# Layer 0's first adaLN shifts on VectorE and its scales on TensorE; the output projection's operands and first tiles made beside the last filter piece

## The chip, the cores and the metric

The kernel runs on one core of a Trainium2 chip. The metric is the device time of one execution in microseconds (us), the median over runs. A core has TensorE (PE in the profile, with its weight loads as PEld), VectorE (DVE), ScalarE (ACT), GpSimd (POOL) and SyncE (SP), which here only issues DMAs. Each works through its own instructions in order and waits on semaphores for the others. All times below are in microseconds from the start of the profiled execution.

## The reference, cut to what matters

A two-layer encoder trunk on a sequence of 1024 tokens with 1024 channels. Layer 0 mixes attention and an RWKV-7 scan, layer 1 is a Hyena operator whose long filters depend on weights alone.

```python
cond = jax.nn.silu(c)
for layer in range(2):
    mod = (cond @ ada_w[layer] + ada_b[layer])[:, None, :]
    shift_m, scale_m, gate_m, shift_f, scale_f, gate_f = jnp.split(mod, 6, axis=-1)
    h = rms_norm(x, norm_mix[layer]) * (1.0 + scale_m) + shift_m
    if layer == 0:
        p = h @ mix_w_in
        y_attn = blocked_gqa(...p...)              # 512 columns
        y_rwkv = rwkv7_bidirectional(...p...)      # 512 columns
        y = jnp.concatenate([y_attn, y_rwkv], axis=-1) @ mix_w_out
    else:
        y = hyena_mixer(h, ...)                    # filters by FFT, from weights alone
    x = x + gate_m * y
    h = rms_norm(x, norm_ffn[layer]) * (1.0 + scale_f) + shift_f
    x = x + gate_f * swiglu(h, ffn_w1[layer], ffn_w3[layer], ffn_w2[layer])
return rms_norm(x, final_norm)
```

The change touches two places of layer 0: `shift_m` and `scale_m` of its first norm, and the first half of the projection by `mix_w_out`, the 512 rows that belong to the attention's output.

## The kernel before

Activations lie in SBUF transposed, as eight tiles of 128 channels by 1024 tokens (`xT`, `h`). The kernel keeps its own stock of SBUF tiles: F32 pages of 128 x 1040 from one end of the memory and F32R pages from the other; `repage(nf, nr)` sets how many there are of each, `page()` takes one and `free()` gives it back, `fence()` sets pages above an index aside. F32R pages hold operands of the large matmuls: every operand is split into a high part (ScalarE, L256) and a low part (VectorE, L257), and `mm3` (L296) multiplies high by high, high by low and low by high. PSUM has eight banks, which `set_banks` divides between two groups. Generators that `yield` are run side by side by `weave`, each with a weight; the order of the program comes from that, and a scheduler of the framework then orders each engine's instructions.

The start: `load_xT` loads x and transposes it on PE (L372). `ada_first` then makes shift (part 0) and scale (part 1) of the first norm: for each half of 512 channels and each part it loads four tiles of `ada_w` (L395) and multiplies each by the condition, as matmuls with one output row (L398, counted twice in the profile, since they are f32). The row is copied (L401), and `ada_cols` turns it into four columns by matmuls with ones (L412), adds the bias (L414) and, for the scale, forms `gs` (L419). All later parts go through `ada_part`, which sums the same products on VectorE in `acc` of 128 x 512 (L441, L443) and lets the ones of L412 sum over the partitions. `norm_h` needs both: L532 multiplies by `gs`, ScalarE (L535) and VectorE (L536) add the shift and split the result. The mixer's first steps then spill x (L206, `sp_x`) and load the input weights (L274). Its first two tiles hold the columns of the decay and learning-rate inputs, whose second products are L1107 and L1109; the weights for these are loaded at L1087.

The end of the mixer: after the input projection, units of the scan (four pairs of heads, two directions; `rwkv_x`, `rwkv_y`, `rwkv_s`, closed by `rwkv_post`) are woven with `other`, which first runs the attention and then `hy_filters`, the filters of layer 1. A filter piece makes taps (PE L1805, ACT L1807, DVE L1808), a first FFT stage (PE L1830, then L1749 to L1751) and, late, an 8-point stage on VectorE (`dft8`, L1699 and L1700), whose result GpSimd stores (L1777). The last stage takes 64 steps of `other` beside the scan's last unit; what is left of it runs alone. Then `repage(13, 33)`, eight loads of x, and `project`: four loads and splits of the attention's outputs (`sp_ya`) and `matvec_add`, which makes for each of eight channel tiles 24 matmuls and two VectorE instructions that add the gated product to x (L801). `ffn` then starts with the second half of the projection, `matvec_halves` (L828), whose operands are the scan's outputs (`sp_yr`).

Of the kernel before, what the change touches and what calls it, by code (L numbers as in the profile page):

```python
# [10 lines left out]
F32 = mybir.dt.float32  # L11
# [65 lines left out]
class Kern:  # L77
# [80 lines left out]

    def free(self, *aps):
        for a in aps:  # L160
            if isinstance(a, (tuple, list)):
                self.free(*a)
            else:
                dt, t, _ = self.page_of[a.tensor.name]
                assert all(t is not q for q in self.pages[dt])
                self.put(t)
# [42 lines left out]
    def unspill(self, d, eng=None):  # L209
        t = self.page()  # L210
        (eng or self.nc.sync).dma_start(out=t, in_=d)
        return t
# [172 lines left out]
    def ada_first(self):  # L385
# [3 lines left out]
        for half in range(2):  # L389
            for part in range(2):  # L390
                c0 = part * D + half * 512
                ps = self.bank()
                for j in range(4):
                    wt = self.page((P, 2, 512))
                    nc.sync.dma_start(out=wt, in_=w[256 * j : 256 * j + 256, c0 : c0 + 512].rearrange("(k p) n -> p k n", p=P))  # L395
                    for i in range(2):
                        k = 2 * j + i
                        nc.tensor.matmul(ps[0:1], self.cond[:, k : k + 1], wt[:, i], start=k == 0, stop=k == 7)  # L398
                    self.free(wt)
                row = self.page((P, 512))  # L400
                nc.scalar.copy(row[0:1], ps[0:1])  # L401
                self.fbank(ps)
                self.ada_cols(0, part, half, row[0:1], 0)
                self.free(row)
# [378 lines left out]
    def matvec_add(self, xT, w, ys, layer, part, g=0, keep=None):  # L783
# [5 lines left out]
        for mp in range(KT // 2):  # L789
# [760 lines left out]
    def mixer(self, w, h, ada):  # L1550
# [120 lines left out]
    def load_mats(self, name):  # L1671

        out = []
        for i in range(2):
            t = self.page((P, 4, 256))
# [78 lines left out]
    def hy_filters(self, g):  # L1754
# [3 lines left out]
        F = self.load_mats("F") + self.load_mats("Fn")  # L1758
# [156 lines left out]
    def hyena(self, w, h, tail):  # L1915
# [140 lines left out]
        def rest():  # L2056
# [5 lines left out]
            for n, _ in enumerate(tail(zs[:4])):  # L2062
                yield 1.0 if n == 0 else 5.3
# [31 lines left out]
def build(ctx, tc, ins, out):  # L2095
# [44 lines left out]
    def project(xT, ys, w, layer, g=0):  # L2140
# [115 lines left out]
```

## Time and profile before

| | before |
|---|---|
| three runs, median | 3384.54 (3375.49 to 3385.33) |
| profiled execution | 3373.19, span 3371.4 |
| mean granted PE clock, profiled execution | 0.963 |
| PE, VectorE, ScalarE, GpSimd busy | 3158.1, 2341.6, 1229.9, 197.0 |
| DMA | 460.24 MB, mean 137 GB/s |

A window's row names its bounds, its length, and per engine the busy time with the count of instructions in brackets; then the granted PE clock, the mean busy share of the 16 DMA engines and their GB/s. A row of the timeline has start, duration, engine, line, operation, output and input, form and count; in brackets at its end stands the idle time of the engine before it and who ended it. A row with "q" behind the engine is an issue, not work. Line numbers in the text are those of the kernel before; in the changed kernel the same lines stand 7 to 19 further down.

### The profile page before, as it was taken

What the parts mean: (1) busy time and instruction counts of PE and PEld (TensorE: products, weight loads), DVE (VectorE), ACT (ScalarE), POOL (GpSimd) and SP (SyncE); (2) the same over time, 40 slices, a digit from 0 to 9 for tenths busy, and PEclk for the clock granted to TensorE, in tenths of its full rate; (3) what the DMA queues carried; (4) which work ended last, traced back from release to release, by engine and by line L of the source; (5) the groups of instructions that cost most, each with busy time, mean ns of one, the idle gap of its engine ahead of it and who ended that gap; (6) DMA issues with size and microseconds to landing.
All of it is one profiled execution on the core that took longest, in us unless ns stands there. A gap on an engine that the chain in (4) does not pass through costs nothing.

```text
span 3371.4 us, 51166 instructions
## 1 busy us (share of the span) xinstructions
PE 3158.1 (94%) x20227; PEld 2554.1 (76%) x20227; DVE 2341.6 (69%) x4011; ACT 1229.9 (36%) x2146; POOL 197.0 (6%) x443
## 2 busy tenths in 40 slices
PE   8899989999989979999999999989977899999998
PEld 4687767776668867888887877877765788888886
DVE  5465565666667895887877665699898686667545
ACT  4632355555554432532233333222120443334211
POOL 2000000000001110000001210000000000000000
PEclk9999999989989999999999999999988999999998
DMA  8654542332334253244449983332446322234311
GB/s 273 220 190 139 158 98 70 84 87 64 76 72 111 98 183 137 94 156 137 147 135 308 352 281 125 100 119 90 148 162 218 132 82 75 77 111 138 122 41 51
DMA packets 331377, 460.24 MB, mean 137 GB/s; under 512 B 101816, under 2 KB 233745, under 8 KB 331136
## 3 DMA queue, kind: packets, MB, share of 16 engines
q1 hardware_dynamic: 292576, 322.04, 31.1%
q0 software_dynamic: 38384, 134.86, 11.4%
q8 instruction: 159, 2.61, 0.3%
q14 instruction: 82, 0.67, 0.1%
q10 hardware_dynamic: 176, 0.07, 0.0%
HBM read 312.71 MB, written 141.56 MB: 135 GB/s over the span
## 4 chain that ended last, share of the span: by engine, by line
PE 58%; DVE 8%; DMA 5%; issue 3%; ACT 2%; POOL 0%; DVEq 0%; SPq 0%; ACTq 0%; POOLq 0%
PE bk L296 21%; PE bk L615 8%; PE bk L616 8%; PE bk L614 8%; PE bk L1830 2%; DVE p L1699 2%; PE bk L1849 2%; DMA p<-in_hy_w_in_dram 1%; DVE p L257 1%; DMA p<-in_ffn_w_dram 1%; PE bk L2002 1%; PE bk L1859 1%; PE bk L1805 1%; PE bk L2025 1%; DMA p<-sp_z 1%
## 5 line engine op out<-in xcount | busy, mean ns | idle before, releaser
L296 PE MATMUL bk<-p,p 128*128 128x512 f32 x5136 | 1235.2, 399 | 75.3 <-ACT p L256 35.0
L296 PEld LDWEIGHTS bk<-p,p 128*128 128x128 f32 x5136 | 974.8, 192 | 299.1 <-ACT p L256 39.3
L256 ACT ACTIVATE p<-p 128x512 fp32r<-128x512 f32 (+3 forms) x542 | 402.6, 758 | 945.8 <-PE bk L615 262.4
L257 DVE TENSOR_TENSOR p<-p,p 128x512 fp32r<-128x512 f32 (+3 forms) x542 | 450.9, 847 | 235.0 <-ACT p L256 189.5
L615 PE MATMUL bk<-p,p 128*128 128x512 f32 x1248 | 485.4, 389 | 3.8 <-DVE p L257 3.8
L614 PE MATMUL bk<-p,p 128*128 128x512 f32 x1248 | 485.0, 390 | 0.1
L616 PE MATMUL bk<-p,p 128*128 128x512 f32 x1248 | 483.8, 389 | 0.0
L615 PEld LDWEIGHTS bk<-p,p 128*128 128x128 f32 x1248 | 234.3, 188 | 53.0 <-DVE p L257 4.7
L614 PEld LDWEIGHTS bk<-p,p 128*128 128x128 f32 x1248 | 234.3, 188 | 48.6 <-ACT p L256 0.5
L616 PEld LDWEIGHTS bk<-p,p 128*128 128x128 f32 x1248 | 234.2, 188 | 48.5
L801 DVE SCALAR_TENSOR_TENSOR p<-bk,mod,p 128x512 f32<-128x512 f32 x192 | 134.9, 744 | 95.0 <-PE bk L296 91.7
L443 DVE SCALAR_TENSOR_TENSOR p<-p,cond,p 128x512 f32<-128x512 f32 x140 | 104.6, 749 | 53.6 <-DMA p<-in_ada_w_dram 51.8
L1699 DVE TENSOR_TENSOR p<-p 128x256 f32<-128x256 f32 (+1 forms) x336 | 130.8, 452 | 0.0
L1830 PE MATMUL bk<-p,p 128*128 128x256 f32 x512 | 125.3, 392 | 5.1 <-DVE p L1751 4.0
L944 DVE TENSOR_REDUCE mx<-bk 128x1 f32<-128x512 f32 x128 | 86.2, 684 | 35.5 <-PE bk L941 34.8
L1830 PEld LDWEIGHTS bk<-p,p 128*128 128x128 f32 x512 | 95.1, 194 | 19.6 <-DVE p L1751 5.1
L1056 ACT COPY p<-bk 128x512 f32<-128x512 f32 (+1 forms) x80 | 43.4, 588 | 169.2 <-DVE p L1876 63.9
L1699 DVE TENSOR_TENSOR p<-p,p 128x1024 f32<-128x1024 f32 (+1 forms) x144 | 91.1, 681 | 18.8 <-ACT p L1850 18.8
L964 ACT COPY p<-bk 128x512 f32<-128x512 f32 x128 | 74.2, 587 | 78.4 <-PE bk L963 75.9
L948 ACT ACTIVATE p<-bk,mx 128x512 f32<-128x512 f32 x128 | 86.9, 686 | 42.3 <-DVE mx L945 41.8
L963 PE MATMUL bk<-k_ident,p 128*128 128x128 f32 x512 | 88.3, 300 | 11.8 <-ACT p L964 9.2
L1362 PEld LDWEIGHTS bk<-p,p 64*64 64x64 f32 x2048 | 73.4, 139 | 29.7 <-issue 15.8
(407 smaller groups left out, 4179.9 us busy)
## 6 DMA issues: line engine op xcount, KB each, us to landing
p<-in_ffn_w_dram SPq DMA_DIRECT2D x120, 512.0 KB, 4.8
p<-in_ada_w_dram SPq DMA_DIRECT2D x96, 512.0 KB, 5.0
sp_f<-p POOLq DMA_DIRECT2D x36, 512.0 KB, 5.5
p<-sp_f POOLq DMA_DIRECT2D x36, 512.0 KB, 5.7
hs<-p POOLq DMA_DIRECT2D x32, 512.0 KB, 3.7
p<-hs SPq DMA_DIRECT2D x32, 512.0 KB, 4.4
p<-sp_r SPq DMA_DIRECT2D x24, 512.0 KB, 5.7
p<-sp_x SPq DMA_DIRECT2D x24, 512.0 KB, 3.6
```

Of the source, the lines that this page charges most:

```text
L256: self.nc.scalar.activation(out=hi, in_=src, func=AF.Copy)
L257: self.nc.vector.tensor_tensor(out=lo, in0=src, in1=hi.bitcast(F32), op=ALU.subtract)
L296: nc.tensor.matmul(ps[n], a, b[:, HALVES[n]], start=s, stop=e)
L443: nc.vector.scalar_tensor_tensor(out=acc, in0=wt[:, i], scalar=self.cond[:, k : k + 1], in1=acc, op0=ALU.mult, op1=ALU.add)
L614: nc.tensor.matmul(ps, op[:, 0, k], mh, start=start and k == 0, stop=False)
L615: nc.tensor.matmul(ps, op[:, 0, k], ml, start=False, stop=False)
L616: nc.tensor.matmul(ps, op[:, 1, k], mh, start=False, stop=stop and k == 3)
L801: nc.vector.scalar_tensor_tensor(out=xs, in0=ps[n], scalar=self.modc(layer, part, m), in1=xs, op0=ALU.mult, op1=ALU.add)
L948: nc.scalar.activation(out=pr[:, HALVES[n]], in_=ps[n], func=AF.Exp, scale=0.125, bias=m[:, 2:3], accum_out=st["s", qt // 4][:, qt % 4, e, ...
L963: nc.tensor.transpose(pt[:, j], pr[:, k * P : (k + 1) * P], self.ident)
L1699: tt = lambda o, a, b, op: nc.vector.tensor_tensor(out=o, in0=a, in1=b, op=op)
L1830: nc.tensor.matmul(ps[j][:, ri], F[2 * d + t2 // 4][:, t2 % 4, 128 * ri : 128 * ri + 128], tp[:, j, d], start=d == 0, stop=d == 1)
```

## The change

In `ada_first` the matmuls L398 stay for the scale alone; the shift is summed on VectorE as in `ada_part`, and the loads of the two parts alternate. The mixer's last stage takes 48 steps of `other` instead of 64, sets pages from 32 on aside, then lowers the stock to 32 F32 pages and raises it to 16 F32R pages, and weaves the rest of `other` with the first six steps of `project`: four loads with their splits, and two tiles. The x tiles of this projection are each loaded at their turn into the lowest free page and kept (`keep`), where before all eight were loaded ahead. The filters' transform matrices are put into low pages too. `project` yields after each split, and the weights of its steps in layer 1 are adapted to that.

```diff
+    def low_page(self, shape=(P, 1024), dt=F32):
+
+        free = self.pages[dt]
+        t = min(free, key=lambda q: self.page_of[q.tensor.name][2])
+        del free[next(i for i, q in enumerate(free) if q is t)]
+        return reshape(t[:, : int(np.prod(shape[1:]))], shape)
...
-    def unspill(self, d, eng=None):
-        t = self.page()
+    def unspill(self, d, eng=None, low=False):
+        t = self.low_page() if low else self.page()
...
     def ada_first(self):
         for half in range(2):
-            for part in range(2):
-                c0 = part * D + half * 512
-                ps = self.bank()
-                for j in range(4):
+            ps, acc, row = self.bank(), self.page((P, 512)), self.page((P, 512))
+            for j in range(4):
+                for part in (1, 0):
+                    c0 = part * D + half * 512
                     wt = self.page((P, 2, 512))
                     nc.sync.dma_start(out=wt, ...)
                     for i in range(2):
                         k = 2 * j + i
-                        nc.tensor.matmul(ps[0:1], self.cond[:, k : k + 1], wt[:, i], start=k == 0, stop=k == 7)
+                        if part:
+                            nc.tensor.matmul(ps[0:1], self.cond[:, k : k + 1], wt[:, i], start=k == 0, stop=k == 7)
+                        elif k == 0:
+                            nc.vector.tensor_scalar(out=acc, in0=wt[:, i], scalar1=self.cond[:, :1], scalar2=None, op0=ALU.mult)
+                        else:
+                            nc.vector.scalar_tensor_tensor(out=acc, in0=wt[:, i], scalar=self.cond[:, k : k + 1], in1=acc, op0=ALU.mult, op1=ALU.add)
                     self.free(wt)
-                row = self.page((P, 512))
-                nc.scalar.copy(row[0:1], ps[0:1])
-                self.fbank(ps)
-                self.ada_cols(0, part, half, row[0:1], 0)
-                self.free(row)
+            nc.scalar.copy(row[0:1], ps[0:1])
+            self.fbank(ps)
+            self.ada_cols(0, 1, half, row[0:1], 0)
+            self.ada_cols(0, 0, half, acc, 0)
+            self.free(row, acc)
...
-    def matvec_add(self, xT, w, ys, layer, part, g=0, keep=None):
+    def matvec_add(self, xT, w, ys, layer, part, g=0, keep=None, low=False):
...
-                x = self.unspill(xT[m]) if away else xT[m]
+                x = self.unspill(xT[m], low=low) if away else xT[m]
...
-    def mixer(self, w, h, ada):
+    def mixer(self, w, h, ada, tail):
...
-            n = (0, 46, 37, 37, 37, 37, 37, 36, 35, 64)[i]
+            n = (0, 46, 37, 37, 37, 37, 37, 36, 35, 48)[i]
+            if i > len(units):
+
+                self.fence(F32, 32)
+                self.zone = (self.pages, self.beyond)
...
-        for _ in other:
-            pass
+        self.zone = (self.pages,)
+        self.repage(32, 16)
+        last = tail([out[i] for i in range(4)])
+        weave((16, other), (6, some(last, 6)))
         self.set_banks(8)
-        return [out[i] for i in range(4)] + [outr[i] for i in range(4)]
+        return last, [outr[i] for i in range(4)]
...
-        F = self.load_mats("F") + self.load_mats("Fn")
+        F = self.load_mats("F", True) + self.load_mats("Fn", True)
...
-                yield 1.0 if n == 0 else 5.3
+                yield 0.3 if n < 4 else 5.3
...
-        y = [K.split(K.unspill(d)) for d in ys]
-        yield
-        yield from K.matvec_add(xT, w, y, layer, 2, g)
+        y = []
+        for d in ys:
+            y.append(K.split(K.unspill(d)))
+            yield
+        yield from K.matvec_add(xT, w, y, layer, 2, g, keep, keep is not None)
...
-    ys = K.mixer(ins["mix_w_in"][0], h, ada)
+    xn = []
+    last, ys = K.mixer(ins["mix_w_in"][0], h, ada, lambda y: project(xd, y, w[:512], 0, 0, xn))
     K.repage(13, 33)
-    xT = [K.unspill(d) for d in xd]
-    run(project(xT, ys[:4], w[:512], 0))
-    xT, steps = K.ffn(xT, halves(xT, ys[4:], w[512:], 0), 0, ada1(), hy_weights(), 20)
+    run(last)
+    xT, steps = K.ffn(xn, halves(xn, ys, w[512:], 0), 0, ada1(), hy_weights(), 20)
```

Three places of the new order. On SP, behind the loads of the adaLN, stand two tables (`k_rope`), the eight spills of x (`sp_x`) and the first loads of the input weights (`mix_w_in`). Before:

```order
L845 DMA p_154<-in_k_rope_s_dram 128x1024
L206 DMA sp_x_700<-p_94 128x1024
L206 DMA sp_x_714<-p_98 128x1024
L274 DMA p_158<-in_mix_w_in_dram 128x8x128
L206 DMA sp_x_740<-p_102 128x1024
L206 DMA sp_x_776<-p_106 128x1024
```

Now, from the last two spills on:

```order
L213 DMA sp_x_941<-p_118 128x1024
L213 DMA sp_x_1009<-p_122 128x1024
L1673 DMA hy_w<-in_hy_f_w_dram 33x64
L1675 DMA hy_w<-in_hy_f_w_dram 64x64 x2
L1673 DMA hy_w<-in_hy_f_w_dram 33x64
L1675 DMA hy_w<-in_hy_f_w_dram 64x64 x2
L114 DMA k_tneg<-in_k_tneg_dram 128x16
L281 DMA p_134<-in_mix_w_in_dram 128x8x128
L281 DMA p_158<-in_mix_w_in_dram 128x8x128
L281 DMA p_82<-in_mix_w_in_dram 128x8x128
```

The first input weight has moved from between the second and the third spill to behind all eight, beside the next two. On VectorE, in layer 0's first norm, L532 and L536 are its passes and the row L257 with three pages is the split of an input weight. Before:

```order
L532 SCALAR_TENSOR_TENSOR p_138<-p_102,gs,bk_65 128x512
L532 SCALAR_TENSOR_TENSOR p_142<-p_106,gs,bk_65 128x512
L257 TENSOR_TENSOR p_238<-p_158,p_234 128x1024
L516 RECIPROCAL rstd_590<-rstd_590 128x4
L414 TENSOR_TENSOR mod<-bk_63,cols 128x4
L536 SCALAR_TENSOR_TENSOR p_514<-p_138,mod,p_510 128x512
L536 SCALAR_TENSOR_TENSOR p_522<-p_142,mod,p_518 128x512
```

Now, at the norm's end (L548 is the former L536, L264 the former L257):

```order
L548 SCALAR_TENSOR_TENSOR p_552<-p_142,mod,p_548 128x512
L1054 TENSOR_SCALAR mu_671<-cols 128x16
L1055 TENSOR_SCALAR mu_672<-cols 128x16
L1057 TENSOR_SCALAR ka_675<-cols 128x4
L1652 TENSOR_TENSOR fb_7622<-cols 128x1
L1652 TENSOR_TENSOR fb_7623<-cols 128x1
L264 TENSOR_TENSOR p_254<-p_134,p_250 128x1024
L264 TENSOR_TENSOR p_238<-p_158,p_234 128x1024
L264 TENSOR_TENSOR p_246<-p_82,p_242 128x1024
```

All three splits stand behind the norm's last pass, where before the first was its seventh row or so. On VectorE at the end of the filters, L1699 and L1700 are the last piece's 8-point stage and L801 closes a tile of the projection. Before:

```order
L1699 TENSOR_TENSOR p_2969<-p_106,p_3009 128x256 x4
L1700 SCALAR_TENSOR_TENSOR p_3029<-p_2961,p_2969 128x256 x2
L1700 SCALAR_TENSOR_TENSOR p_150<-p_2961,p_2969 128x512 x2
L1700 SCALAR_TENSOR_TENSOR p_3029<-p_2961,p_2969 128x256 x2
L257 TENSOR_TENSOR p_10878<-p_82,p_10874 128x1024
L257 TENSOR_TENSOR p_10926<-p_130,p_10922 128x1024
L257 TENSOR_TENSOR p_10862<-p_102,p_10858 128x1024
L257 TENSOR_TENSOR p_10830<-p_106,p_10826 128x1024
L257 TENSOR_TENSOR p_10854<-p_122,p_10850 128x1024
L801 SCALAR_TENSOR_TENSOR p_126<-bk_65,mod,p_126 128x512
L801 SCALAR_TENSOR_TENSOR p_126<-bk_66,mod,p_126 128x512
```

Now, where the first two tiles are closed (L813 is the former L801; L1769 and L1770, formerly L1750 and L1751, are the first FFT stage, of which this is the last piece):

```order
L1719 SCALAR_TENSOR_TENSOR p_2991<-p_98,p_2979 128x256 x2
L1770 SCALAR_TENSOR_TENSOR p_106<-p_154,bk_65 128x512
L1769 TENSOR_TENSOR p_2975<-p_126,bk_66 128x512
L1770 SCALAR_TENSOR_TENSOR p_2963<-p_126,bk_66 128x512
L813 SCALAR_TENSOR_TENSOR p_94<-bk_63,mod,p_94 128x512
L813 SCALAR_TENSOR_TENSOR p_94<-bk_64,mod,p_94 128x512
L1769 TENSOR_TENSOR p_2995<-p_114,bk_65 128x512
L1770 SCALAR_TENSOR_TENSOR p_106<-p_114,bk_65 128x512
L264 TENSOR_TENSOR p_10730<-p_154,p_10726 128x1024
L813 SCALAR_TENSOR_TENSOR p_98<-bk_68,mod,p_98 128x512
L813 SCALAR_TENSOR_TENSOR p_98<-bk_70,mod,p_98 128x512
```

The first L801 stood five splits behind the last L1700; now the first two tiles are closed among the rows L1750 and L1751 of the last piece, ahead of its 8-point stage, and two more tiles before that stage ends.

More of the change, by code (lines that the diff above doesn't have):

```diff
@@ L1669, in hy_hidden, with load_mats @@
         return hid
-    def load_mats(self, name):
+    def load_mats(self, name, low=False):
         out = []
         for i in range(2):
-            t = self.page((P, 4, 256))
+            t = (self.low_page if low else self.page)((P, 4, 256))
             self.nc.gpsimd.dma_start(out=t, in_=self.ins["k_" + name][:, 4 * i : 4 * i + 4, :])
@@ L2138, in build, with project @@
     K.ada_first()
-    def project(xT, ys, w, layer, g=0):
-        y = [K.split(K.unspill(d)) for d in ys]
-        yield
-        yield from K.matvec_add(xT, w, y, layer, 2, g)
+    def project(xT, ys, w, layer, g=0, keep=None):
+        y = []
[3 more added lines that the diff above has]
+        yield from K.matvec_add(xT, w, y, layer, 2, g, keep, keep is not None)
         K.free(y)
```

## The prediction

> **What bounds the kernel now.** I read the page first, then the windows, then the timeline of the two places that the change touches.
>
> ```profile
> span 3371.4 us, 51166 instructions
> PE 3158.1 (94%) x20227; PEld 2554.1 (76%) x20227; DVE 2341.6 (69%) x4011; ACT 1229.9 (36%) x2146; POOL 197.0 (6%) x443
> core 0: us, PE busy (x) PEld busy (x) DVE busy (x) ACT busy (x) POOL busy (x), PEclk, DMA share, GB/s
> 18.00:42.00 24.00, 23.75 (x78) 7.47 (x79) 9.60 (x20) 9.72 (x18) 4.76 (x19) 1.00 1.04 368
> 84.00:105.00 21.00, 12.34 (x33) 7.70 (x34) 10.99 (x9) 19.41 (x27) 0.88 (x5) 0.67 0.56 178
> 600.00:1150.00 550.00, 508.37 (x6560) 398.21 (x6559) 366.55 (x821) 301.65 (x666) 35.66 (x69) 0.93 0.32 82
> 1230.00:1280.00 50.00, 30.52 (x141) 23.11 (x140) 46.15 (x82) 15.37 (x16) 4.35 (x9) 0.80 0.81 292
> 1280.00:1317.00 37.00, 37.00 (x163) 30.58 (x163) 18.05 (x23) 5.94 (x6) 0.00 (x0) 1.00 0.24 75
> ```
>
> The mean says TensorE, busy 94% of the span. The windows say where that is untrue. From 18 to 42 us the DMA engines are full (share 1.04): the start is paced by loads. From 1230 to 1280, where the mixer ends, VectorE is busy 46.15 of 50 us while PE is idle 19.5 us at a granted clock of 0.80; right behind it PE is full and VectorE half idle. The first place is that of the adaLN edit, the second that of the projection edit. Between them, over 600 to 1150, PE is idle 41.6 us in holes of the scan, which the change does not address.
>
> **Part 1, the first adaLN.** What is removed is half of the matmuls with one output row, L398.
>
> ```profile
> 18.25 10.46 PE L398 MATMUL bk<-p,cond 128*1 128x512 f32 x24 [0.45 <-ACT p L373]
> 41.43 8.74 PE L398 MATMUL bk<-p,cond 128*1 128x512 f32 x20
> L443 DVE SCALAR_TENSOR_TENSOR p<-p,cond,p 128x512 f32<-128x512 f32 x140 | 104.6, 749 | 53.6 <-DMA p<-in_ada_w_dram 51.8
> 7.12 22.09 SPq L395 DMA_DIRECT2D p<-in_ada_w_dram  x16
> p<-in_ada_w_dram SPq DMA_DIRECT2D x16, 512.0 KB, 11.6
> ```
>
> 32 of 64 matmuls at 8.74/20 = 0.437 us go: 14.0 us of PE. VectorE gets 16 passes of 0.749 us, 12.0 us, in a stretch where it worked 9.60 of 24 us. The loads stay: 16 in 22.09 us, 1.38 us each, so the last is issued at 29.2 and lands about 40.8 (plus 11.6). The last two passes end near 42.3; before, PE was at L398 until 50.2. That lets layer 0's norm start earlier:
>
> ```profile
> 59.56 2.72 DVE L532 SCALAR_TENSOR_TENSOR p<-p,gs,bk 128x512 f32<-128x512 f32 x4
> 74.92 1.42 DVE L536 SCALAR_TENSOR_TENSOR p<-p,mod,p 128x512 fp32r<-128x512 f32 x2
> 41.77 0.53 SPq L274 DMA_DIRECT2D p<-in_mix_w_in_dram  x1
> 58.03 1.02 SPq L274 DMA_DIRECT2D p<-in_mix_w_in_dram  x2
> p<-in_mix_w_in_dram SPq DMA_DIRECT2D x3, 512.0 KB, 4.4
> 69.33 14.11 PE L296 MATMUL bk<-p,p 128*128 128x512 f32 x61 [1.09 <-DVE p L257]
> 90.87 1.22 PE L1107 MATMUL bk<-p,p 128*128 128x512 f32 x2 [7.43 <-DVE p L1091]
> 99.25 0.50 PE L1107 MATMUL bk<-p,p 128*128 128x512 f32 x1
> 101.12 4.12 ACT L1112 ACTIVATE p<-bk,cols 128x512 f32<-128x512 f32 x7
> 1300.00:1310.00 10.00, 10.00 (x46) 8.27 (x45) 2.12 (x4) 0.00 (x0) 0.00 (x0) 1.00 0.01 2
> ```
>
> The norm is 32 VectorE passes (L532, L536) of 0.68 to 0.71 us. By the new order four of them stand ahead of the last adaLN pass, so 28 x 0.70 = 19.6 us follow, and with a microsecond each for the modulation and for small ones the norm ends near 64 instead of 76.3 (74.92 + 1.42). But the reordering takes something back. The first input weight, issued at 41.77 among the spills of x, now stands behind all of them with the two that went at 58.03: one transfer less ahead, so at 58.03 - 1.38 = 56.7, there by 61.1. And its split stands on VectorE behind the whole norm, so it ends near 65 (1.22 us, row below). Only then does PE begin the first two tiles, 96 matmuls, of which it had done 35 before 69.33. At 10/46 = 0.217 us they take 20.9 us; a cold start costs 3.4 more (24 matmuls in 2.07 + 6.56 = 8.63 us behind the idle time at 1263, against 5.2). So L1107 comes at 89.3 instead of 90.87: 1.6 us. The load of the decay weights, which ended the 7.43 us stall, follows the norm's end and is 12 us earlier, so PE waits for itself there. Behind it eight pairs L1107/L1109 took 8.4 us up to 99.25; at ScalarE's 4.12/7 = 0.59 us a pair they need 4.7. Of these 3.7 us I take two thirds, since the first pairs also wait for their activation. Sum: **4 us** gained. Bounds: no cold start and all of the pairs, 1.6 + 3.4 + 3.7 = 8.7; two more transfers ahead of the weights (2.8) and no gain in the pairs, -1.2.
>
> The Trainium skill, "TensorE: Matmul & The Clock Gate", section "Part 1: The HAM clock gate", has a rule against this edit: after idling the array runs at half rate until it has been busy for about 3.4 us. Taking matmuls out of 18 to 50 us leaves PE mostly idle ahead of its first dense stage. By that rule the cold start would cost an estimated 1.7 us and the sum for this part would be about 6; the row at 1263 measured twice as much, and I go by the row.
>
> **Part 2, the projection begun beside the filters.** The rows of before:
>
> ```profile
> 1211.08 0.41 DVE L1812 TENSOR_TENSOR p<-p,skip 1x256 f32<-1x256 f32 x1
> 1215.91 1.89 PE L1830 MATMUL bk<-p,p 128*128 128x256 f32 x8
> 1251.84 0.32 SPq L206 DMA_DIRECT2D sp_yr<-p  x1
> 1252.98 1.22 DVE L257 TENSOR_TENSOR p<-p,p 128x1024 fp32r<-128x1024 f32 x1 [1.17 <-ACT p L256]
> 1263.33 2.07 PE L296 MATMUL bk<-p,p 128*128 128x512 f32 x4 [10.32 <-ACT p L256]
> 1266.37 6.56 PE L296 MATMUL bk<-p,p 128*128 128x512 f32 x20 [0.96 <-DVE p L257]
> 1268.71 2.63 DVE L1700 SCALAR_TENSOR_TENSOR p<-p,p 128x256 f32<-128x256 f32 x6
> 1275.49 44.85 PE L296 MATMUL bk<-p,p 128*128 128x512 f32 x188 [2.56 <-ACT p L256]
> 1315.62 1.41 DVE L801 SCALAR_TENSOR_TENSOR p<-bk,mod,p 128x512 f32<-128x512 f32 x2 [4.03 <-PE bk L296]
> ```
>
> The first half of the projection is 8 tiles of 24 matmuls, each closed by two L801; the last L801 ends at 1317.0. By 1271.3, when VectorE is done with the filters, PE has almost one tile behind it. In the new order four tiles' L801 stand ahead of the filters' last row on VectorE. Nothing is added or removed there, so I count when each engine could close tile 8.
>
> VectorE: from the same filter row (L1812, 1211.08) it needs 60.3 us to the filters' end before. Now 7 more splits of 1.22 us, 8 L801 of 0.70 and three L1808 of 0.6 stand in between, 15.9 us, so 1287.2; then 8 more L801 and about 4.5 splits, 11.1 us: 1298.3. That is 18.7 us ahead of 1317.0. PE: the low half of the first weight is split just ahead of the norm of the last scan output, which ends at 1251.8; 184 matmuls from there are 39.9 us, the cold start 3.4, the last 8 filter matmuls 1.9, and the second weight pair, whose page frees some 4 us later, keeps it about 3: 1300, and with its two L801 1301.4. That is 15.6 ahead. Counting only tiles closed by VectorE at 1281 (four now, two before) gives 49 matmuls, 10.6 us. I take **14 us**, near the PE count, less a wait or two that neither count holds. Bounds: 5.2, if the two tiles named in the call are all that is gained over the one that ran already; 18.7 by VectorE. The splits of the second half, which came at 1280 to 1294, are hidden behind PE's remaining tiles; their cover is the half idle VectorE of 1280 to 1317, and without it they cost the 11.1 us above. The x tiles were loaded eight ahead and are kept in both; no bytes change.
>
> **The rest.** Scan rows move by a few places; nothing is added. Its 41.6 us of holes fall on eight units, 5.2 each: I take 0, and 5.2 either way. The Hyena weights (0.3, 5.3) only shift splits of a projection that PE hides.
>
> Sum: 4 + 0 + 14 = **18 us** from the profiled execution's 3373.2 gives 3355. The median of the three runs is 11.3 us above that execution, so beside runs like them I expect 3384.5 - 18 = **3366.5**. A measurement of this kernel can tell about 0.3%, 10.2 us, from no change.
>
> **Rivals.**
>
> ```profile
> p<-sp_yr SPq DMA_DIRECT2D x4, 512.0 KB, 6.6
> p<-in_mix_w_out_dram SPq DMA_DIRECT2D x8, 512.0 KB, 4.7
> 1260.00:1270.00 10.00, 5.71 (x13) 4.02 (x14) 10.00 (x21) 4.23 (x4) 0.53 (x1) 0.50 0.99 375
> ```
>
> *Loads take the place of the splits.* On SP seven of the eight x tiles and three weights, 512 KB each, now stand behind the spill of the last scan output (1251.84). At 375 GB/s of a full DMA (0.99) these ten are 14.0 us. If three of them then cost VectorE a landing of 4.7 us each, 14.1 us, the 14 are gone and the whole is 4: 3380.5, no measurable change. For it: the full DMA. Against: the loads are spread over four tiles' time.
> *The scan gives it back.* Two units' holes double: 10.4 us, 18 becomes 8, 3377. For it: many rows moved; against: all of it is small swaps.
> *Slower.* L801 stands inside VectorE's filter order, so an x tile or a weight that is late stops the filters as well, and with them PE, which works in order. If six of the eight tiles each wait a landing of 6.6 us there, 39.6 us, tile 8 closes at 1338, 21 later than before; with the 4 us of the start the whole is 17 slower, 3401. It decides from the fifth wait on (33 us against 18.7 + 4 + 10.2). Against: loads would have to come one by one.
> *It does not do what it says* is out: the order shows both edits done.
>
> **How the numbers follow.** Forecast 0.69, loads 0.15, scan 0.07, slower 0.09. Faster by over 0.3% is the forecast, 0.69; within 0.3% the two middle ones, 0.22; slower 0.09. The range: gains of 8.7 + 5.2 + 18.7 = 32.6 down to -1.2 - 5.2 + 5.2 = -1.2 give 3352 to 3386; that holds the two middle rivals and leaves out the slower one and some of the tails.
>
> **What would show it.** Right: L398 32 times; the norm's last L536 near 64 and L1107 near 89; the last filter row on VectorE near 1287 less the 4 us gained, with four tiles closed; the eighth tile closed some 18 us earlier than 1317; equal lengths behind it. Wrong: VectorE idle beside L801 for x or a weight; PE still waiting at 90; scan units of other lengths.

## The result, and the profile after

The changed kernel was faster, by about as much as predicted. It was measured twice, each time beside runs of the kernel before; three of the four runs of before in the first row are those shown ahead of the prediction.

| | before, median (runs) | changed, median (runs) | ratio, 95% interval |
|---|---|---|---|
| first | 3384.57 (3375.49 to 3385.33, 4) | 3355.89 (3348.07 to 3367.59, 4) | 0.9927 [0.9902, 0.9953] |
| again | 3378.03 (3367.34 to 3387.64, 21) | 3362.88 (3350.85 to 3373.90, 8) | 0.9952 [0.9931, 0.9972] |

The ratios are 24.7 and 16.2 us of 3384.57 and 3378.03 (a ratio here is not the quotient of the two medians, which lie 28.7 and 15.2 us apart); the prediction was 18 us less and 3366.5, between 3352 and 3386. The profiled executions themselves differ far less, 3373.19 and 3367.59: the one of before lay below all four of its runs, the one of the change is the slowest of its four. So a single pair of profiles says little about the sum here, and the stages have to be read one by one, in more than one profile.

The page of the changed kernel, its first lines:

```profile
span 3365.7 us, 51134 instructions
PE 3154.6 (94%) x20195; PEld 2559.1 (76%) x20195; DVE 2349.2 (70%) x4027; ACT 1231.5 (37%) x2144; POOL 197.4 (6%) x443
```

The windows of the changed kernel (columns as ahead of the prediction), the first three over the same times as there, the fourth where the mixer ends now:

```profile
18.00:42.00 24.00, 21.42 (x72) 8.89 (x72) 19.99 (x38) 9.97 (x19) 3.60 (x15) 0.79 1.04 367
84.00:105.00 21.00, 17.81 (x64) 12.81 (x62) 8.62 (x7) 17.42 (x24) 0.62 (x2) 0.84 0.53 174
600.00:1150.00 550.00, 507.05 (x6502) 395.52 (x6499) 360.06 (x810) 296.54 (x652) 32.34 (x63) 0.92 0.31 80
1245.00:1295.00 50.00, 46.55 (x234) 39.73 (x235) 44.74 (x71) 14.93 (x18) 2.23 (x5) 0.93 0.64 225
```

VectorE took the work over at the start (19.99 busy instead of 9.60 us), the loads still fill the DMA engines (1.04), but PE's granted clock there fell from 1.00 to 0.79. At the mixer's end PE is busy 46.55 of 50 us, where it was 30.52.

To compare stages of the same work I cut the span at three instructions that stand in every kernel: the first matmul of the input projection's third tile (PE, 104.72 before), one filter row near the scan's end (VectorE, L1808 at 1047.19) and one row just behind the mixer (VectorE, L494 at 1328.24). Each window then holds the same matmuls (their count stands in brackets; it differs by up to 30 in a few kernels where rows crossed a bound), so its length less PE's busy time is PE's idle time, and in the rows below a longer busy time for the same count goes with a lower granted clock (875.90 us at 0.95, 893.32 at 0.93). Before:

```profile
104.72:1047.19 942.47, 875.90 (x9123) 683.72 (x9123) 570.31 (x1164) 469.24 (x968) 35.47 (x86) 0.95 0.42 114
1047.19:1328.24 281.05, 257.09 (x2078) 213.56 (x2075) 228.21 (x438) 102.24 (x196) 31.21 (x57) 0.96 0.37 130
1328.24:3371.40 2043.16, 1940.67 (x8714) 1608.92 (x8712) 1489.17 (x2325) 603.98 (x902) 112.01 (x244) 0.97 0.43 142
```

The changed kernel, first profile:

```profile
105.51:1061.92 956.41, 887.34 (x9123) 690.84 (x9123) 568.64 (x1164) 470.23 (x968) 35.70 (x88) 0.94 0.41 112
1061.92:1329.81 267.89, 256.73 (x2078) 214.72 (x2075) 227.31 (x438) 101.54 (x196) 31.23 (x57) 0.97 0.39 137
1329.81:3365.73 2035.92, 1935.26 (x8714) 1604.64 (x8712) 1489.56 (x2325) 605.76 (x902) 112.27 (x244) 0.97 0.43 142
```

So in this pair the start is 0.8 us later, the input stage and scan 13.9 longer, the mixer's end 13.2 shorter and the rest 7.2 shorter. The mixer's end is where the projection was edited; 13.2 stands beside the predicted 14. The rest holds only the adapted weights of the projection's steps in layer 1. In the profiles below it is 2.0 and 3.4 us shorter in two kernels without that edit (the adaLN alone, and both parts on PE), and 3.1 and 4.4 in two with it (the projection alone, and the change's second profile), so it is not shown that the 7.2 belong to the edit. The start and the scan are what the experiments had to explain.

The start, in the changed kernel's timeline (SP, VectorE and PE):

```profile
56.53 2.27 SPq L281 DMA_DIRECT2D p<-in_mix_w_in_dram  x3
64.17 0.74 DVE L548 SCALAR_TENSOR_TENSOR p<-p,mod,p 128x512 fp32r<-128x512 f32 x1
65.19 3.49 DVE L264 TENSOR_TENSOR p<-p,p 128x1024 fp32r<-128x1024 f32 x3
64.56 2.07 PE L303 MATMUL bk<-p,p 128*128 128x512 f32 x4 [16.46 <-ACT p L263]
67.60 23.68 PE L303 MATMUL bk<-p,p 128*128 128x512 f32 x92 [0.96 <-DVE p L264]
91.11 0.62 PE L1119 MATMUL bk<-p,p 128*128 128x512 f32 x2
```

The weight was issued at 56.53 (predicted 56.7), the norm ended at 64.9 (predicted 64), and PE waits for nothing at 91. But the 96 matmuls took from 64.56 to 91.28, 26.7 us, where 20.9 and a cold start of 3.4 were predicted; 0.96 of the 26.7 is a wait for the low half of the first weight.

The mixer's end, on VectorE and PE (L813 closes a tile, L1719 is the filters' last pass):

```profile
1275.56 1.41 DVE L813 SCALAR_TENSOR_TENSOR p<-bk,mod,p 128x512 f32<-128x512 f32 x2 [0.32 <-PE bk L303]
1304.89 2.62 DVE L1719 SCALAR_TENSOR_TENSOR p<-p,p 128x256 f32<-128x256 f32 x6
1320.13 0.74 DVE L813 SCALAR_TENSOR_TENSOR p<-bk,mod,p 128x512 f32<-128x512 f32 x1
1285.28 40.04 PE L303 MATMUL bk<-p,p 128*128 128x512 f32 x175
```

PE is without a hole from 1285.28 on, 22 us ahead of the filters' end on VectorE (1307.5). In the kernel before, its dense stretch began at 1275.49, 4 us behind the filters' end. Counted from the last but one of the filter rows L1812 (1211.08 before, L1831 at 1225.09 here), the eighth tile closes after 95.79 us instead of 105.95. In absolute time it closes at 1320.9 and not 18 us ahead of 1317, since the scan has become longer; scan units of other lengths were among the signs named for a wrong prediction.

### The profile page after: what moved, and what is told of

Its sections match the earlier page's. It is cut to its first block, busy times and chain, and to the rows that moved or that the text cites. A ratio compares the mean times of both kernels' runs of the same rounds, so it can differ in the third digit from the quotient of the medians.

```text
span 3365.7 us, 51134 instructions
## 1 busy us (share of the span) xinstructions
PE 3154.6 (94%) x20195; PEld 2559.1 (76%) x20195; DVE 2349.2 (70%) x4027; ACT 1231.5 (37%) x2144; POOL 197.4 (6%) x443
## 4 chain that ended last, share of the span: by engine, by line
PE 70%; DVE 12%; DMA 9%; ACT 4%; issue 3%; SPq 1%; POOL 0%; DVEq 0%; ACTq 0%; POOLq 0%
PE bk L303 25%; PE bk L626 8%; PE bk L628 8%; PE bk L627 8%; DMA p<-in_hy_w_in_dram 2%; DVE p L1718 2%; PE bk L1849 2%; PE bk L1868 2%; PE bk L1310 2%; PE bk L1374 2%; DVE p L264 2%; PE bk L975 1%; PE bk L996 1%; PE bk L952 1%; DMA p<-in_mix_w_in_dram 1%
## 5 line engine op out<-in xcount | busy, mean ns | idle before, releaser
L264 DVE TENSOR_TENSOR p<-p,p 128x512 fp32r<-128x512 f32 (+3 forms) x542 | 450.9, 847 | 255.4 <-ACT p L263 211.7
L813 DVE SCALAR_TENSOR_TENSOR p<-bk,mod,p 128x512 f32<-128x512 f32 x192 | 134.9, 744 | 71.8 <-PE bk L303 69.1
L1068 ACT COPY p<-bk 128x512 f32<-128x512 f32 (+1 forms) x80 | 43.5, 589 | 182.1 <-PE bk L303 68.4
L504 ACT ACTIVATE p<-p 128x512 f32<-128x512 f32 x80 | 50.0, 632 | 121.1 <-DVE p L840 111.3
```

Of the source, the lines that this page charges most:

```text
L264: self.nc.vector.tensor_tensor(out=lo, in0=src, in1=hi.bitcast(F32), op=ALU.subtract)
L813: nc.vector.scalar_tensor_tensor(out=xs, in0=ps[n], scalar=self.modc(layer, part, m), in1=xs, op0=ALU.mult, op1=ALU.add)
```

## The experiments

Each was measured beside runs of the kernel before on the same chip; the number of runs stands in brackets. Where two kernels ran on different chips, their ratios to before are compared. In the text "start" is the time of the third tile's first matmul.

**One part alone.** The adaLN alone is the kernel before with the changed `ada_first`; the projection alone is the changed kernel with the former one, so its diff is the same lines the other way round. The first of the two, to the kernel before:

```diff
...
-                        nc.tensor.matmul(ps[0:1], self.cond[:, k : k + 1], wt[:, i], start=k == 0, stop=k == 7)
+                        if part:
+                            nc.tensor.matmul(...)
+                        elif k == 0:
+                            nc.vector.tensor_scalar(out=acc, ...)
+                        else:
+                            nc.vector.scalar_tensor_tensor(out=acc, ...)
...
```

> Only the first adaLN is changed; the projection is as before. Theory of the prediction: the norm ends 11 us earlier, L1107 (here L1119) comes 1 to 2 us earlier and the pairs gain 2.5, so 4 us less than before (about 3380). Rival, from the profile of the changed kernel, where L1119 came at 91.11 and the scan's input stream was 0.8 us late by 105: the first weights, late on SP, take it all, so 0 (3384), and the whole gain belongs to the projection.

Measured: 3383.93 (12 runs) beside 3377.93 (23), 1.0018 [1.0005, 1.0030]: slower by 6 us, which neither theory had. Its windows:

```profile
101.44:1064.15 962.71, 893.32 (x9123) 694.30 (x9123) 569.08 (x1164) 469.32 (x968) 35.45 (x86) 0.93 0.41 112
1064.15:1344.80 280.65, 256.55 (x2078) 213.22 (x2075) 228.09 (x438) 102.09 (x196) 31.20 (x57) 0.96 0.37 131
```

The start is 3.3 us earlier (101.44), nearly the predicted 4, and here the 96 matmuls took what was forecast (24.3 with the cold start):

```profile
63.43 24.12 PE L296 MATMUL bk<-p,p 128*128 128x512 f32 x96 [18.70 <-ACT p L256]
```

The mixer's end is as before (280.65). The loss lies between: 20.2 us more over the input stage and the scan. PE's idle time grew by 2.8 us (69.4 beside 66.6); its busy time for the same 9123 matmuls grew by 17.4. The mean granted clock of the 12 runs was 0.958, of the 23 runs of before 0.9614.

> Only the projection is changed (with its steps in layer 1); the first adaLN is as before. Theory of the prediction: 14 us less than before (3370), tile 8 closed some 14 us earlier after the same filter row. Rival: the projection is the whole of the measured 28.7 us between the medians, adaLN nothing: 3356 to 3360. If this and the adaLN alone together give well under the whole, something that belongs to neither, such as the scan's own order, makes the rest.

Measured: 3360.58 (5), 0.9956 [0.9940, 0.9971], 14.9 us less in the whole time: near the predicted 14, and not the 28.7 of the rival. Its windows:

```profile
104.93:1044.65 939.72, 874.03 (x9123) 680.57 (x9123) 569.92 (x1164) 469.73 (x968) 35.67 (x88) 0.95 0.41 115
1044.65:1317.09 272.44, 255.06 (x2078) 212.04 (x2075) 227.44 (x438) 101.17 (x196) 31.14 (x57) 0.97 0.38 135
```

But the edited stage is not 14 us shorter here. The mixer's end is 8.6 us shorter, and the eighth tile closes 99.75 us after the same filter row (L1826 at 1208.96, the former L1812), 6.2 earlier than before where 14 was expected. The other 5.7 of the 14.3 us between the two profiles lie in the scan (2.8) and behind the mixer (3.1), less 0.2 at the start. PE is idle 17.4 us at the mixer's end, 7.66 of them in one wait:

```profile
1247.72 0.39 SPq L281 DMA_DIRECT2D p<-in_mix_w_out_dram  x1
1254.24 1.06 ACT L263 ACTIVATE p<-p 128x1024 fp32r<-128x1024 f32 x1 [7.61 <-DMA p<-in_mix_w_out_dram]
1255.35 3.78 PE L303 MATMUL bk<-p,p 128*128 128x512 f32 x8 [7.66 <-ACT p L263]
```

The first weight of the projection was late, 6.5 us from its issue to ScalarE's split (3.5 in the changed kernel, 1261.87 to 1265.36). ScalarE waited for it, and PE for ScalarE. That is, in part, the prediction's first rival, loads in the place of the splits. The kernel with the former adaLN and early first weights (below) has a wait of 1.09 us in that place, so it does not come with the former adaLN as such; why it came here is open.

Start and scan are within 3 us of those of before. This kernel and the one with the adaLN alone differ in the order of rows between the start and the mixer's end: with the projection alone PE's rows up to the scan's last units stand as in the kernel before, while the adaLN's edit put more than a thousand of the 9123 PE rows of the input stage and the scan into other places, though none was added or removed there.

**The changed kernel again**, unedited.

> The changed kernel itself, beside the same runs of before as the next three, and a second profile of it. If the two parts add up as measured alone (1.0018 and 0.9956 of before), 0.9974. If the adaLN is worth its 4 us behind the projection's, 0.993 or less. Its input stage ends within a microsecond of before's in the first profile (106.2 and 107.0); the scan of 644 us in that profile should come out shorter if it was a matter of this one run.

Measured: 0.9952 [0.9931, 0.9972], given above. That lies between the two values named, at the projection alone (0.9956): behind it, the adaLN adds nothing that can be seen, with intervals that leave some 9 us either way.

```profile
105.26:1057.44 952.18, 882.50 (x9123) 686.39 (x9123) 568.09 (x1164) 469.13 (x968) 35.66 (x88) 0.94 0.41 113
1057.44:1323.17 265.73, 251.88 (x2078) 209.92 (x2075) 227.41 (x437) 101.28 (x196) 31.15 (x57) 0.99 0.39 138
```

The scan did not come back to before's 942 us, and the mixer's end is 15.3 us shorter than before. The eighth tile closes 93.63 us after the filter row (1220.61), 12.3 earlier than before.

**How many steps beside the filters.** Four operands without a tile, and four operands with four tiles, where the change has four with two.

```diff
-        weave((16, other), (6, some(last, 6)))
+        weave((16, other), (6, some(last, 4)))
```

```diff
-        weave((16, other), (6, some(last, 6)))
+        weave((16, other), (8, some(last, 8)))
```

> The changed kernel with the four operands made beside the filters' last piece, but no tile. Theory of the prediction: PE's count of matmuls ahead of the filters' end makes the gain, so the two tiles are worth 48 matmuls, 10.4 us, less what PE still fits in: 5 to 10 us slower than the changed kernel (3361 to 3366). Rival: the operands alone make the gain, since PE is full behind them and its tiles fill holes in any order: within 2 us of the changed kernel.

Measured: 3370.79 (12), 0.9976 [0.9963, 0.9989], some 8 us slower than the changed kernel's second result, as predicted for the two tiles, though the two intervals overlap a little.

> The changed kernel with eight steps of the projection beside the filters' last piece, four operands and four tiles, where it has six. If PE's matmuls ahead of the filters' end make the gain, as the two tiles made (0.9976 without them), two more are worth up to 10 us less what the loads and weights hold up: 3 to 8 us less than the changed kernel. Rival: the next weights and VectorE's own filter rows bind, and L813 between them delays the filters: no gain, or some microseconds slower.

Measured: 3363.70 (8), 0.9957 [0.9941, 0.9972]: the rival, no gain. The mixer's end of both, operands only first:

```profile
1046.49:1318.89 272.40, 255.24 (x2078) 211.64 (x2075) 227.78 (x437) 101.27 (x196) 31.25 (x57) 0.98 0.38 135
```

```profile
1060.14:1326.29 266.15, 257.26 (x2090) 215.44 (x2087) 227.34 (x438) 101.30 (x196) 31.14 (x57) 0.97 0.40 139
```

281.05 with nothing beside the filters, 272.40 with the operands, 267.89 and 265.73 with two tiles, 266.15 with four. PE's idle time there goes 24.0, 17.2, 11.2 and 13.9, 8.9. The projection alone, also with two tiles, does not fit this row: 272.44 and 17.4, by the wait shown above. What was to be had by two more tiles had been had: from VectorE's last but one filter row L1831 (1223.29) to the second half's first closed tile (1319.56) the kernel with four tiles takes 96.3 us, with no idle PE after the last L1831 at all; the changed kernel, from 1220.61 to 1316.36 in its second profile, takes 95.8.

**Is it the matmuls taken from PE?** The kernel before with the loads alternating as in the change, and both parts still on PE.

```diff
-            for part in range(2):
-                ps = self.bank()
-                for j in range(4):
+            ps = [self.bank() for _ in range(2)]
+            for j in range(4):
+                for part in (1, 0):
...
-                        nc.tensor.matmul(ps[0:1], ...)
+                        nc.tensor.matmul(ps[part][0:1], ...)
...
```

> Before, with the adaLN's loads alternating between scale and shift as in the change, but both summed on PE: the 16 VectorE passes are gone and the 32 matmuls are back. If the adaLN alone was slower because the taken matmuls leave PE cold at the start and in the scan (clock 0.958 against 0.9614 of before), this is as fast as before or faster, 3374 to 3379 by the runs of before so far, clock 0.961. If it was the order of rows in the input stage and the scan, sorted anew by any edit at the start, this is slower as well, 3382 to 3386 with a clock near 0.958.

Measured: 3398.88 (6), 1.0061 [1.0040, 1.0083], clock 0.9607: slower than either condition said, with the clock near that of the first and the time beyond that of the second. Its start is 2.7 us later than before, and then:

```profile
107.40:1077.85 970.45, 882.12 (x9123) 685.24 (x9123) 572.34 (x1164) 474.28 (x970) 35.46 (x86) 0.94 0.41 111
```

28.0 us more than before between start and scan's end, 21.7 of it idle PE (88.3 beside 66.6). Nothing in that stage was edited, and the matmuls had been left on PE. So an edit at the start can lengthen the scan without taking a matmul from PE. What the two slower kernels share is that each has its rows in a new order, not the same one; and this one loses by idle PE, where the adaLN alone lost by a lower clock. So this run does not show why the clock was lower there. But a low clock in the scan is no fixed consequence of the taken matmuls: with them taken and almost the same order of rows, six profiles have 0.93 to 0.95 in that window, before 0.95.

**The order alone.** The changed kernel with PSUM's banks put back, behind the first adaLN, into the turn that they had before. No work changes; the rows come into a third order, not back into that of before.

```diff
     K.ada_first()
+    banks = sorted(K.banks[0], key=lambda q: (int(q.tensor.name[2:].split("_")[0]) - 1) % 8)
+    K.banks[0].clear()
+    K.banks[0].extend(banks)
```

> The changed kernel with PSUM's eight banks put back, behind the first adaLN, into the turn that they have in before. No work changes; rows of the input stage and the scan are sorted anew once more. If what the adaLN takes back in the scan hangs on the order that the edit happened to make, the scan's idle time of PE (57 us in three profiles of the change) moves by 5 us or more, and the whole with it, either way. If the scan only scatters from run to run with PE's clock, idle stays at 54 to 59 and the ratio inside 0.993 to 0.997.

Measured: 3374.44 (12), 0.9990 [0.9977, 1.0003], 13 us slower than the changed kernel's second result. The whole moved, out of 0.993 to 0.997, as the first condition has it. PE's idle time hardly moved by the window below, 71.5 us beside 69.1 and 69.7 of the changed kernel; the 57 of the expectation is of a shorter window, whose bounds are not given, so that part of the condition stays undecided:

```profile
100.61:1061.55 960.94, 889.48 (x9123) 689.42 (x9123) 569.57 (x1164) 470.61 (x968) 35.71 (x88) 0.94 0.41 112
```

Its busy time, 889.48, lies inside the 872.5 to 893.3 us that the changed order alone took in six profiles. So this profile does not show where the 13 us are.

**The first weights first.** The changed kernel with the first two input weights loaded and split right behind the adaLN's loads.

```diff
-        if ahead is not None:
+        if ahead is not None and ahead not in self.ahead:
...
-    low = [K.page(dt=F32R) for _ in range(10)]
+    for c0 in (768 + 12 * P, 768 + 13 * P)[:2]:
+        K.ahead[c0] = K.load_w(ins["mix_w_in"][0][:, c0 : c0 + P], KT, P)
+    low = [K.page(dt=F32R) for _ in range(6)]
```

> The changed kernel, with the first two input weights loaded and split right behind the first adaLN's loads, instead of behind the spills of x and the Hyena constants. If PE's wait for the first weight (until 64.56) takes the adaLN's gain, PE starts ten or more us earlier and L1119 comes near 80 instead of 91: 8 us or more less than the changed kernel (3348 beside 3356). Rival: the norm's end at 64.9 and what follows on VectorE and ScalarE bind anyway: L1119 within 3 us of 91, no difference.

Measured: 3353.18 (6), 0.9930 [0.9915, 0.9945]. Its timeline on PE:

```profile
45.94 18.14 PE L303 MATMUL bk<-p,p 128*128 128x512 f32 x68
64.06 6.62 PE L303 MATMUL bk<-p,p 128*128 128x512 f32 x28
77.87 1.22 PE L1119 MATMUL bk<-p,p 128*128 128x512 f32 x2 [7.19 <-DVE p L1103]
```

PE starts 18.6 us earlier, follows the norm tile by tile, and L1119 comes at 77.87 instead of 91.11, the start at 91.71 instead of 105.51. So it was the first weight's place on SP that held the start back. That the whole is 8 us less than the changed kernel, as expected with it, is not shown: 0.9930 beside 0.9927 and 0.9952.

> The projection's change and the early first weights, with the adaLN of before on PE. If the shift on VectorE is worth something once the weights don't wait, this is slower than the kernel with both and early weights (0.993 of before) by the later norm, some 4 to 10 us: 0.995 to 0.996. Rival: the shift on VectorE only trades PE time for cold PE time: 0.993 or less.

(As the one above, with the former `ada_first`.) Measured: 3369.39 (12), 0.9981 [0.9967, 0.9995]. Its start is at 99.81. So with early weights the shift on VectorE is worth 8.1 us of start (99.81 to 91.71; 6.3 to the second profile below, 93.47), where it was worth -0.8 to 3.3 with late ones. The whole is some 17 us slower than with both (0.9981 beside 0.9930), more than the 4 to 10 expected; most of the remaining distance lies in the scan, 959.24 beside 945.92 us.

> The kernel with the early first weights (0.993), with the banks put back in the same way. If its gain over the changed kernel is that of the start, where L1119 came 13 us earlier, the ratio stays at 0.991 to 0.995. If it was a lucky order of the scan (632 us with 65.5 us of cold PE in its profile, beside 640 to 649), the ratio goes back to 0.995 or more with the start as early as before.

(Early weights and the banks put back.) Measured: 3379.47 (12), 1.0003 [0.9989, 1.0017]. The start kept its place, 92.96, and the mixer's end too, 266.81; the whole gain was lost between:

```profile
92.96:1067.98 975.02, 888.13 (x9133) 691.93 (x9134) 570.46 (x1164) 470.64 (x967) 35.80 (x88) 0.94 0.40 110
```

> The kernel with the early first weights once more, with its own order of rows. If an order of rows keeps its worth from run to run, the ratio is again 0.991 to 0.995 and the scan's idle time near 57 us with 65 to 85 us of cold PE. If its first result was the luck of its runs, it comes out at 0.997 or more, nearer to the same kernel with the banks put back (1.0003).

Measured: 3349.67 (6) beside 3376.77 (11), 0.9924 [0.9900, 0.9947], on another chip: no luck of its runs. Its row beside the last one:

```profile
93.47:1037.53 944.06, 875.66 (x9144) 680.54 (x9144) 568.56 (x1164) 471.17 (x968) 36.45 (x88) 0.96 0.42 114
```

The same work but for 11 matmuls at a bound, 31.0 us apart, 18.5 of it idle PE (86.9 beside 68.4). The ratios say the same of the whole time, 0.9930 and 0.9924 against 1.0003, some 24 to 27 us with intervals well apart. Nothing differs but the turn of the banks and the order of rows that came of it. This version has the lowest median of all; whether it beats the changed kernel was not measured side by side, and the intervals overlap.

**A warm start.** The changed kernel with 28 matmuls of finished norm tiles, read by nobody, ahead of the first weight.

```diff
+    for m in range(2, 6):
+        ps = K.bank()
+        hi = h[m][0]
+        for q in range(7):
+            K.nc.tensor.matmul(ps, hi[:, :P], hi[:, HALVES[q % 2]], start=True, stop=True)
+        K.fbank(ps)
```

> The changed kernel with 28 extra matmuls of the norm's finished tiles (their sums are read by nobody) between the adaLN's last matmul and the first weight's arrival. If the clock is what takes the adaLN's gain at the start, PE comes warm to its first 96 matmuls: they take 20.9 us instead of 26.7 in the profile, L1119 comes at 86 to 87 instead of 91.1, cold time up to there falls from 41 to some 25 us, and the whole is 4 to 6 us less than the changed kernel (0.9935 to 0.994 of before beside 0.9952 and 0.9927). Rival: the input stage and the scan behind it are bound elsewhere and absorb it: L1119 earlier, the whole unchanged.

Measured: 3364.59 (9), 0.9959 [0.9945, 0.9972], L1119 at 91.03: no change at the start. But the test missed its aim. Its timeline on PE, and its window behind it:

```profile
50.03 9.70 PE L2179 MATMUL bk<-p 128*128 128x512 f32 x28 [2.33 <-ACT p L547]
64.54 2.07 PE L303 MATMUL bk<-p,p 128*128 128x512 f32 x4 [4.59 <-ACT p L263]
67.57 23.62 PE L303 MATMUL bk<-p,p 128*128 128x512 f32 x92 [0.96 <-DVE p L264]
```

```profile
64.00:92.00 28.00, 26.50 (x101) 21.14 (x102) 12.20 (x17) 11.35 (x13) 0.20 (x2) 0.84 0.40 94
```

PE was idle for 4.59 us between the extra work and its first tile, and the clock behind was 0.84. The changed kernel's row for the same window, without them, has the same clock:

```profile
64.00:92.00 28.00, 26.48 (x100) 21.19 (x101) 12.23 (x18) 11.30 (x13) 0.20 (x2) 0.84 0.39 94
```

Ahead of it, over 50 to 64 us, the granted clock was 0.74 with the extra matmuls and 0.50 without. So the test does not show what a warm PE brings at the start. Another profile with the start unedited, that of the kernel with four tiles, comes nearer to it:

```profile
63.36 24.18 PE L303 MATMUL bk<-p,p 128*128 128x512 f32 x96 [19.15 <-ACT p L263]
64.00:92.00 28.00, 26.21 (x106) 20.69 (x104) 10.57 (x10) 14.48 (x17) 0.29 (x3) 0.93 0.44 107
```

There the clock over 64 to 92 was 0.93, L1119 came at 87.38 and the start at 101.43, 3.8 and 4.1 us ahead of the changed kernel's first profile. The Trainium skill, "TensorE: Matmul & The Clock Gate", section "Part 1: The HAM clock gate", says that one window of about 3.4 us without work is enough to halve the clock; an idle time of 4.59 us that undid 9.70 us of work agrees with it.

## Why the prediction held

*The projection, 14 us: right in the whole time, less clearly in the stage that it was counted for.* Alone it measured 14.9 us. By stage the mixer's end is 13.2 and 15.3 us shorter in two profiles of the change, but 8.6 with the projection alone. The eighth tile, which the count was made for, closes 10.2, 12.3 and 6.2 us earlier after the same filter row in these three. PE's count, 15.6, was nearer than VectorE's, 18.7, which was not reached, since VectorE ends the filters at 1307.5 and still waits for PE and ScalarE between. The mechanism, PE's hole filled ahead of the filters' end, is borne out by the steps: the operands alone give 8.6 us of the stage, two tiles up to 15.3, and with four tiles nothing more is left, because PE has no hole any more. The first rival's loads were late indeed, on ScalarE. In the changed kernel PE had other matmuls meanwhile; with the projection alone it had none and waited 7.66 us. The waits of the changed kernel between the last but one L1831 and the eighth tile (who waited for whom: total, times, longest):

```profile
ACT p L263 <- DMA p<-in_mix_w_out_dram: 19.0, 3, 13.4
DVE p L264 <- ACT p L263: 8.6, 4, 3.6
DVE p L1769 <- PE bk L1849: 3.6, 1, 3.6
PE bk L303 <- ACT p L263: 0.7, 1, 0.7
```

*The first adaLN, 4 us: the mechanism was right, the term for the clock not a fixed one, and the net in the whole time is nothing that can be seen.* Issue, norm's end and the removed stall came as worked out. The 96 matmuls, forecast at 24.3 us, took 24.1 and 24.2 in two profiles with this start (the adaLN alone and the kernel with four tiles) and 26.7 in three others, the change's two among them, where the clock over 64 to 92 us was 0.84 or 0.85. The start moved with it: 3.3 us the right way in the first two, 0.8 and 0.5 the wrong way in the change's two profiles; all lie inside the bounds given (-1.2 to 8.7). The pairs behind the 96 matmuls, where 2.5 us were expected, gained nothing in either case: 14.4 us from L1119 to the third tile (91.11 to 105.51), 14.1 with the adaLN alone (87.39 to 101.44), 13.9 before. In the whole time the edit is worth nothing that can be seen behind the projection (0.9952 beside 0.9956), and alone it costs 6 us, which lie in the next step.

*"Scan rows move by a few places; nothing is added", 0 with 5.2 either way: wrong in size.* The edit at the start moved more than a thousand PE rows. The changed order has 956.4 and 952.2 us there, and almost the same order with other tails, with the warm start or alone 941.8, 958.7, 946.1 and 962.7; before's order has 942.5 and 939.7. So one order scatters by 21 us between profiles, its mean is some 12 us above that of before, and its lowest is as low as before's: the cost of this order is likely, its size is not settled. An order can do far more than 5.2: two orders of one kernel lay 31.0 us apart there, and some 24 to 27 in the whole time. The rival "the scan gives it back" named the place and the price, 10.4 us, but by idle time in two units. In the changed kernel's two profiles idle time grew by 2.5 and 3.1 us only; 11.4 and 6.6 us are busy time at a clock of 0.94 instead of 0.95.

So the total was right partly by luck, by sums that cancel: the start gave less than forecast in the change's own profiles, the scan took some back, and the stage behind the mixer was 4 to 7 us shorter, which was not forecast and is not shown to come from the edit. The measured 16.2 is the projection's 14.9 with what is left over. The first measurement's 24.7 is 8 us above it, within the intervals of both.

What is not settled: which rows of an order cost the time. The windows show it as idle PE in some orders and as a lower clock in others, spread over the scan; no single wait was tested.

## What to carry to other kernels

Work taken off an engine that waits for loads is not a gain until the next stage can start, so look first at what that stage waits for: here the first weight stood behind spills and small tables, and moving two loads was worth 12 to 14 us of start, where the edit itself gave -0.8 to 3.3; how much of that reaches the whole time was not measured side by side. Fill a hole of PE only until it is closed: operands and two tiles all but closed this one, two more tiles brought nothing. And where rows are sorted anew by any edit, measure the edit under a second order of the same work, and read its stage in more than one profile, before crediting or blaming it.

## What the runs showed of the hardware that was not expected

The same program scatters by 0.7% here: 81 runs of the kernel before lie between 3364.74 and 3388.61 us. Their time goes with the granted clock: over the 23 runs beside the first four experiments a fitted line gives 2.7 us for 0.001 of mean clock, and the 12 runs of the adaLN alone give nearly the same slope, 2.8. The same 9123 matmuls in almost the same order took 872.5 to 893.3 us of busy PE in six profiles, with 64 to 74 us of idle time. At the start, the same first 96 matmuls of the input projection took 24.2 us in one profile (the kernel with four tiles) and 26.7 in the changed kernel's two. The Trainium skill's "TensorE: Matmul & The Clock Gate", section "Part 1: The HAM clock gate", says that the window by which the clock is decided runs freely, so that the same kernel meets it in another phase each time; the scatter fits that, though no run here set the phase.
